# A hybrid S5 / Conformer layer on one core: every other gate weight tile moved into an 8 KB buffer and prepared a tile ahead, and the rest of the adaLN modulation computed as rows

## Chip, core and metric

The kernel is written in Bass/Tile and runs on one core of one Trainium2 chip. The metric is the device time of one execution in microseconds. The engines are called PE (TensorE, matrix products), DVE (VectorE), ACT (ScalarE), POOL (GpSimd) and SP (SyncE, which here only issues DMAs; ACT issues the stores).

## What is computed

One layer of a network on 2048 tokens of 1024 channels, with a context prefix of 256 tokens, all in float32. Cut to what matters for the change:

```python
mod = silu(c) @ ada_w + ada_b                 # 6 parts of 1024: sh1 sc1 g1 sh2 sc2 g2
nl  = modulate(rmsnorm(x, norm1_g), sh1, sc1)
zl  = nl @ w_in          # 512 S5 input | 1024 conv GLU input | 2048 branch gate logits
ys  = s5_mixer(zl[:, :512], ...)              # bidirectional state-space scan, 32 groups
ya  = s5_glu_out(ys, w_glu, w_a)
yb  = conformer_branch(zl[:, 512:1536], ...)  # a*sigmoid(b), conv of width 31, LayerNorm, silu, @ w_b
x   = x + g1 * (sigmoid(ga) * ya + sigmoid(gb) * yb) @ w_out
nl2 = modulate(rmsnorm(x, norm2_g), sh2, sc2)
out = rmsnorm(x + g2 * conv_ffn(nl2, w_up, dw, w_down), final_g)
```

## The kernel before

A float32 product is made of three PE products of rounded halves: `split` (L446 to L453) rounds an operand to a high half (a cast on ACT, L449) and takes the rest as a low half (a subtraction on DVE, L453), and `mm3` (L459 to L464) multiplies high by high (L462), high by low (L463) and low by high (L464). A tile of 128 output channels by 512 tokens takes 8 slices of the contraction, so 24 matmuls of 512 columns; a tile of 128 channels over all 2048 tokens is four such blocks.

The program runs in stages: the first modulation parts and the S5 input (0 to about 345 us), then the conv GLU tiles and the gates with the S5 scans and the convolution behind them (to about 850 us), the two branch outputs and the merge (phase 3a, 850 to 1150 us), the output projection, and the FFN (1330 us to the end).

**Gates and GLU tiles (L826 to L872).** `v_pair(ct)` computes one channel tile of the conv GLU: four blocks whose sigmoid goes into a tile `av` (L840, ACT), then four blocks that are multiplied into it (L847, DVE), and a store of `av` to DRAM on ACT's queue (L849). `gate(m)` computes one channel tile of gate logits, takes its sigmoid and stores it. The order is v_pair(0), gates 0 to 2, v_pair(1), gates 3 to 5, v_pair(2), gates 6 and 7, v_pair(3), gates 8 to 13; gates 14 and 15 come last with a pool of their own (`ring2`).

**Weights.** `wtile` (L498 to L510) loads two pieces of 256 KB into `w_raw` (three buffers, on SP, L496), and splits each into a `w_ch` of the pool `ring`, which has three slots. A weight tile takes two of the three, so of the next tile one half can be prepared, and the other waits until PE has read the first half of the present one for the last time.

**The S5 in the background (L337 to L412).** After each block of 24 matmuls a `background` call lets the S5 generator take three steps and the convolution 0.75 of one. For each of 32 groups SP loads a record `grp` of three parts (L348, L349, L350); two matmuls read it (L385), POOL and DVE rotate and scan (L394 to L397, L408, L410), POOL rotates back (L361 to L364), and three kinds of matmul read out (L368 to L370). The convolution reads `av` back from DRAM (`caw`, L784, on SP) with its weights `ctw` (L781).

**Buffers.** Tiles of 8 KB per partition share one tag, `z8`, with eight buffers. During the gates four hold a normalised input block; the other four serve `av` and `grp`. A tile takes the buffer that came free longest ago, in program order, and the loads of SP stand in one queue, so a load that waits for its buffer holds up all that stand behind it.

**Rest of the modulation (L890 to L937).** The last four parts are done in phase 3a: `ada_rest` loads `ada_w` in slabs (L924) and accumulates them on DVE (L928); `collect` (L901 to L917) sums over the 128 partitions with PE. Parts 0 and 3 (the two gates g1, g2) come as a row: one matmul with a vector of ones over 512 columns (L907), the bias loaded as a row (L908), an addition (L909) and a store to the DRAM row `d_row` (L910). Parts 1 and 2 (shift and scale of the second modulation) come as columns: four matmuls of one column each (L913) and one addition (L917).

The lines which the diff touches, and the gate loop that calls them:

Of the kernel before, what the change touches and what calls it, by code (L numbers as in the profile page):

```python
# [9 lines left out]
F32 = mybir.dt.float32  # L10
F32R = mybir.dt.float32r
I32 = mybir.dt.int32
AF = mybir.ActivationFunctionType
OP = mybir.AluOpType
# [3 lines left out]
D = 1024  # L18
SEQ = 2048
# [411 lines left out]
class Net:  # L431
# [91 lines left out]
    def run(self):  # L523
        nc, tc = self.nc, self.tc
        with ExitStack() as ctx:
            self.cp = cp = ctx.enter_context(tc.tile_pool(name="const", bufs=1))
            dp = ctx.enter_context(tc.tile_pool(name="scratch", bufs=1, space=DRAM))
            dt_ = lambda nm, sh: dp.tile(sh, F32, name=nm)
            self.scr = {
                "rec": dt_("d_rec", [G, 128, 512 + 2 * NX]), "kd": dt_("d_kd", [G, H, 2 * T - 1, H]),  # L530
                "u": dt_("d_u", [G, H, T, NX]), "y": dt_("d_y", [G, H, T, NCL]),
                "sg": dt_("d_sg", [2, 8, 128, SEQ]), "cv": dt_("d_cv", [4, 128, CS, CX]),
                "av": [dt_(f"d_av{i}", [128, CS, CX]) for i in range(4)],
                "mg": [dt_(f"d_mg{b}", [8, 128, 512]) for b in range(4)], "h": dt_("d_h", [16, 128, D]),
                "hid": dt_("d_hid", [22, 128, SEQ]), "row": dt_("d_row", [2, D]),
                "m8": cp.tile([128, G], F32, name="m8"),
            }
            cp.tile([128, 8], F32, name="align")
            self.big = ctx.enter_context(tc.tile_pool(name="big", bufs=1))
            self.phase1()  # L540
            self.phase3b_4()
            self.phase5()
# [54 lines left out]
    def phase1(self):  # L597
        nc, tc, ins, scr, v, a = self.nc, self.tc, self.ins, self.scr, self.v, self.a
        w_in = ins["w_in"]
        with ExitStack() as ctx:  # L600
            psum = ctx.enter_context(tc.tile_pool(name="ps1", bufs=4, space=PSUM))
            up = ExitStack()
            ring = up.enter_context(self.pool("ringu", 8))
# [148 lines left out]
            ring = ringx.enter_context(self.pool("ring", 3))  # L752
# [3 lines left out]
            stage = []  # L756
# [52 lines left out]
            def background(nconv=None, ns5=None):  # L809
                if nconv is None:  # L810
                    nconv = 0.75
                if ns5 is None:
                    ns5 = 3.0
                pace[0] += nconv
                while pace[0] >= 1.0:
                    pace[0] -= 1.0
                    while fill:
                        try:
                            next(fill[0])
                            break  # L820
                        except StopIteration:
                            fill.pop(0)
                pace[1] += ns5
                while pace[1] >= 1.0:
                    pace[1] -= 1.0
                    next(s5, None)  # L826
# [3 lines left out]
            def v_pair(ct):  # L830
# [18 lines left out]
                self.store(scr["av"][ct], av)  # L849
                fill.append(conv_rows(ct))  # L850

            def gate(m, order=(0, 1, 2, 3), w=None):
                w = w or self.wtile(ring, w_in, 1536 + 128 * m)
                for b in order:
                    ps = psum.tile([128, 512], F32, name="ps", tag="mm")
                    self.gemm(ps, w, x_of(b))
                    sg = evp.tile([128, 512], F32, name="sgg", tag="ev")
                    with self.urgent():
                        a.activation(sg, ps, AF.Sigmoid)
                    self.store(scr["sg"][m // 8][m % 8][:, 512 * b:512 * b + 512], sg)  # L860
                    background()

            m = 0
            for ct in range(4):
                v_pair(ct)
                for _ in range((3, 3, 2, 0)[ct]):
                    gate(m)
                    m += 1
            while m < 14:
                gate(m)  # L870
                m += 1
# [21 lines left out]
    def ada_rest(self, psum, fp):  # L893

        v, cp, pe = self.v, self.cp, self.pe
        self.A2 = cp.tile([128, 8], F32, name="A2")
        self.S2 = cp.tile([128, 8], F32, name="S2")
        ar = Arena([self.z8("ada", [128, 2048])])
        accs, slabs = [ar(128, 512) for _ in range(2)], [ar(128, 512) for _ in range(2)]

        def collect(j, acc):  # L901
            c0 = 2048 + 512 * j
            part, hf = j // 2, j % 2
            ps = psum.tile([128, 512], F32, name="ps", tag="mm")
            if part in (0, 3):
                row = fp.tile([1, 512], F32, name="adrow")
                pe.matmul(ps[0:1, :], self.ones[:, 0:1], acc, start=True, stop=True)  # L907
                self.dma(row, self.ins["ada_b"][None, c0:c0 + 512])  # L908
                v.tensor_tensor(row, row, ps[0:1, :], op=OP.add)  # L909
                self.dma(self.scr["row"][part // 3:part // 3 + 1, 512 * hf:512 * hf + 512], row)  # L910
            else:
                for i in range(4):
                    pe.matmul(ps[:, i:i + 1], acc[:, 128 * i:128 * i + 128], self.ones[:, 0:1],  # L913
                              start=True, stop=True)
                dst = self.S2 if part == 1 else self.A2
                i0 = c0 // 128
                v.tensor_tensor(dst[:, 4 * hf:4 * hf + 4], ps[:, :4], self.col["ab"][:, i0:i0 + 4], op=OP.add)  # L917

        for j in range(8):
            c0 = 2048 + 512 * j  # L920
            acc = accs[j % 2]
            for k in range(8):
                sl = slabs[k % 2]
                self.dma(sl, self.ins["ada_w"][128 * k:128 * k + 128, c0:c0 + 512])  # L924
                if k == 0:
                    v.tensor_scalar(acc, sl, self.sc[:, 0, 0:1], None, op0=OP.mult)
                else:
                    v.scalar_tensor_tensor(acc, sl, self.sc[:, k, 0:1], acc, op0=OP.mult, op1=OP.add)  # L928
                if k % 2:
                    yield  # L930
                if k == 5 and j:
                    collect(j - 1, accs[(j - 1) % 2])
        yield
        yield
        collect(7, accs[1])
        v.scalar_tensor_tensor(self.A2, self.A2, 1.0, self.col["n2"], op0=OP.add, op1=OP.mult)
        yield  # L937
# [329 lines left out]
    def phase5(self):  # L1267
        nc, tc, ins, scr, v, a = self.nc, self.tc, self.ins, self.scr, self.v, self.a
        RES = 18
        with ExitStack() as ctx:  # L1270
# [5 lines left out]
            g2 = op_.tile([128, D], F32, name="g2row", bufs=1)  # L1276
# [39 lines left out]
            def down(t0, nt, nlast):  # L1316

                n = 128 * nt
                acc = [[psum.tile([128, 512], F32, name="ps", tag="mm") for _ in range(2)] for _ in range(nt)]

                pair = []

                def operand(k):
                    hr = hp.tile([128, n], F32, name="hr", bufs=2)
                    self.dma(hr, scr["hid"][k][:, 128 * t0:128 * t0 + n])
                    if not pair:
                        t = hp.tile([128, 2, 512], F32R, name="hhl")
                        pair.extend(t[:, :, o:o + n] for o in range(0, 512, n))
                    ht = pair.pop(0)
                    self.split(ht[:, 0], ht[:, 1], hr)  # L1330
                    return ht, wk(k)

                def step(x, j, hf, i):
                    (ht, w), js = x, slice(128 * j, 128 * j + 128)
                    self.mm3(acc[j][hf], (ht[:, 0, js], ht[:, 1, js]), w[hf], i == 0, i == 21)

                for i, k in enumerate(ORDER[:22 - nlast]):
                    x = operand(k)
                    for j in range(nt):
                        for hf in range(2):  # L1340
                            step(x, j, hf, i)
                if t0 == 0:
                    self.dma(fg, ins["final_g"][None, :].to_broadcast([128, D]))
                    self.dma(g2, scr["row"][1:2, :].to_broadcast([128, D]))
                xs = [operand(k) for k in ORDER[22 - nlast:]]
                for j in range(nt):
                    for hf in range(2):
                        for i, x in enumerate(xs):
                            step(x, j, hf, 22 - nlast + i)
                    residual(t0 + j, acc[j])  # L1350

            for t0, nt, nlast in ((0, 4, 2), (4, 4, 2), (8, 4, 2), (12, 2, 2), (14, 2, 6)):
                down(t0, nt, nlast)
# [58 lines left out]
```

## Time and profile before

| | |
|---|---|
| three runs, median (lowest to highest) | 2812.69 us (2808.87 to 2816.03) |
| the profiled execution's own time | 2806.18 us |
| its span | 2804.4 us |
| mean granted PE clock | 0.984 of full speed |
| PE busy | 2711.9 us, 97% of the span, 12044 matmuls |
| DVE busy | 1508.0 us, 54% |
| ACT busy | 822.7 us, 29% |
| POOL busy | 459.3 us, 16% (nearly all of it before 850 us) |
| chain that ended last | PE 75%, DVE 9%, DMA 6%, POOL 5% |

PE is busy for 97% of the span, and of the rest only a part lies in the two stages that the change touches. The rows below therefore look at single waits of PE in the stretch of the gates, and at the queues on which those waits hang. In a timeline row the first number is the start and the second the duration in microseconds; a bracket at the end gives the idle time of the engine before the row and what ended it. A matmul row lasts longer than the distance to the next start, since matmuls overlap.

### The profile page before, as it was taken

To read this page: it belongs to the slowest core of one execution; us is meant where nothing else is said; L and a number is where in the kernel's file an instruction comes from. 1 tells how busy PE (TensorE), PEld (TensorE's weight loads), DVE (VectorE), ACT (ScalarE), POOL (GpSimd) and SP (SyncE) were. 2 spreads that over 40 slices of the span, in tenths; PEclk is the share of its full clock that TensorE was granted. 3 is DMA by queue.
4 is the path that set the end of the run, shared out by engine and by line. 5 is a ranking of instruction groups with operands and counts; after the bars stand their busy time and mean duration, and the time that the engine had idled before them with its cause. 6 is when DMAs were issued, how large, how long until landed. Compare 5 with 4: busy or idle time off the path is not lost.

```text
span 2804.4 us, 32119 instructions
## 1 busy us (share of the span) xinstructions
PE 2711.9 (97%) x12044; PEld 2203.2 (79%) x12044; DVE 1508.0 (54%) x2312; ACT 822.7 (29%) x1446; POOL 459.3 (16%) x504
## 2 busy tenths in 40 slices
PE   7998999999999999999999999999999989999998
PEld 3786878788887777788888888888888878787887
DVE  5867643433316788566855646556465462414154
ACT  2555412121235443243421222212222132212122
POOL 2256477667600000000000000000000000000000
PEclk8999999999999999999999999999999999999999
DMA  8645745354436576533111111111111153323143
GB/s 315 195 142 165 205 138 153 126 177 147 145 102 202 173 206 200 187 131 113 64 46 57 42 49 49 49 53 46 45 57 42 53 179 107 113 71 135 53 143 98
DMA packets 327308, 334.73 MB, mean 119 GB/s; under 512 B 95336, under 2 KB 240360, under 8 KB 324464
## 3 DMA queue, kind: packets, MB, share of 16 engines
q1 hardware_dynamic: 245680, 235.13, 27.2%
q10 hardware_dynamic: 81472, 97.54, 10.0%
q8 instruction: 95, 1.56, 0.2%
q14 instruction: 61, 0.50, 0.1%
HBM read 230.38 MB, written 102.21 MB: 119 GB/s over the span
## 4 chain that ended last, share of the span: by engine, by line
PE 75%; DVE 9%; DMA 6%; POOL 5%; issue 2%; ACT 2%; SPq 0%; ACTq 0%; POOLq 0%; DVEq 0%
PE ps L464 23%; PE ps L462 23%; PE ps L463 23%; DMA sgab<-d_sg 2%; PE ps L795 1%; DVE Hs L408 1%; PE ps L577 1%; PE ps L385 1%; POOL t L395 1%; DVE Hs L410 1%; DMA slab<-in_ada_w_dram 1%; DMA ada<-in_ada_w_dram 1%; POOL t L394 1%; POOL t L361 1%; PE ps L1112 0%
## 5 line engine op out<-in xcount | busy, mean ns | idle before, releaser
L1242 DVE SCALAR_TENSOR_TENSOR acc<-pad,fw,acc 128x1024 f32<-128x1024 f32 x352 | 450.4, 1282 | 238.9 <-ACT acc L1238 229.5
L477 POOL TENSOR_TENSOR rs_y<-rs_v,mhalf 128x1 f32<-128x1 f32 (+1 forms) x41 | 27.4, 668 | 2048.8 <-DVE rs_v L476 2048.8
L462 PE MATMUL ps<-wd,hhl 128*128 128x512 f32 x704 | 275.6, 393 | 13.5 <-ACT hhl L449 7.3
L463 PE MATMUL ps<-wd,hhl 128*128 128x512 f32 x704 | 275.7, 392 | 0.0
L464 PE MATMUL ps<-wd,hhl 128*128 128x512 f32 x704 | 275.3, 392 | 0.1
L408 DVE TENSOR_TENSOR_SCAN Hs<-m,S 64x287 f32<-64x287 f32 x64 | 68.8, 1075 | 240.5 <-POOL S L396 240.1
L453 DVE TENSOR_TENSOR hhl<-hr,hhl 128x512 fp32r<-128x512 f32 (+1 forms) x110 | 63.0, 582 | 244.4 <-ACT hhl L449 244.1
L453 DVE TENSOR_TENSOR w_ch<-w_raw,w_ch 128x512 fp32r<-128x512 f32 x134 | 106.4, 801 | 137.9 <-ACT w_ch L449 137.5
L462 PEld LDWEIGHTS ps<-wd,hhl 128*128 128x128 f32 x704 | 133.2, 189 | 43.3 <-ACT hhl L449 7.9
L449 ACT CAST w_ch<-w_raw 128x512 fp32r<-128x512 f32 x142 | 87.6, 621 | 267.2 <-PE ps L464 167.1
L463 PEld LDWEIGHTS ps<-wd,hhl 128*128 128x128 f32 x704 | 133.2, 189 | 28.6 <-DVE wd L453 1.0
L464 PEld LDWEIGHTS ps<-wd,hhl 128*128 128x128 f32 x704 | 133.1, 189 | 28.5 <-DVE hhl L453 0.8
L449 ACT CAST hhl<-hr 128x512 fp32r<-128x512 f32 (+1 forms) x110 | 57.2, 534 | 264.5 <-PE ps L464 231.3
L463 PE MATMUL ps<-nm2l,w_ch 128*128 128x512 f32 x344 | 133.8, 389 | 0.0
L464 PE MATMUL ps<-nm2h,w_ch 128*128 128x512 f32 x344 | 133.8, 389 | 0.0
L462 PE MATMUL ps<-nm0h,w_ch 128*128 128x512 f32 x344 | 133.8, 389 | 0.0
L463 PE MATMUL ps<-nm0l,w_ch 128*128 128x512 f32 x344 | 133.8, 389 | 0.0
L463 PE MATMUL ps<-nm1l,w_ch 128*128 128x512 f32 x344 | 133.8, 389 | 0.0
L463 PE MATMUL ps<-nm3l,w_ch 128*128 128x512 f32 x344 | 133.8, 389 | 0.0
L464 PE MATMUL ps<-nm0h,w_ch 128*128 128x512 f32 x344 | 133.8, 389 | 0.0
L462 PE MATMUL ps<-nm1h,w_ch 128*128 128x512 f32 x344 | 133.8, 389 | 0.0
L464 PE MATMUL ps<-nm1h,w_ch 128*128 128x512 f32 x344 | 133.8, 389 | 0.0
(370 smaller groups left out, 6354.5 us busy)
## 6 DMA issues: line engine op xcount, KB each, us to landing
w_raw<-in_ffn_w_up_dram SPq DMA_DIRECT2D x88, 256.0 KB
d_hid<-acc ACTq DMA_DIRECT2D x88, 256.0 KB
w_raw<-in_ffn_w_down_dram SPq DMA_DIRECT2D x76, 256.0 KB
grp<-d_rec SPq DMA_DIRECT2D x32, 576.0 KB
hr<-d_hid SPq DMA_DIRECT2D x66, 256.0 KB
d_sg<-sgg ACTq DMA_DIRECT2D x64, 256.0 KB
ada<-in_ada_w_dram SPq DMA_DIRECT2D x64, 256.0 KB
sgab<-d_sg SPq DMA_DIRECT2D x32, 512.0 KB
```

The costliest lines, as they stand in the source:

```text
L361: g_.tensor_tensor(r1, Hl, tb[:, 0:1, LAT].to_broadcast([128, 2, NCL]), op=OP.mult)
L385: nc.tensor.matmul(ps[:, :NX], sm[:, i, :], ug, start=True, stop=True)
L394: g_.tensor_tensor(t1, S, tb[:, 0:1, :].to_broadcast([128, 2, NX]), op=OP.mult)
L395: g_.tensor_tensor(t2, S[:, ::-1, :], tb[:, 1:2, :].to_broadcast([128, 2, NX]), op=OP.mult)
L408: v.tensor_tensor_scan(Hs[0:64, i, 1:1 + nsc], mb[0:64], S[0:64, i, 0:nsc], 0.0, op0=OP.mult, op1=OP.add)
L410: v.tensor_tensor_scan(Hs[64:128, i, NX - 1 - nsc:NX - 1][:, ::-1], mb[64:128], S[64:128, i, NX - nsc:NX][:, ::-1], 0.0, op0=OP.mult, op1= ...
L449: self.a.copy(hi, src)
L453: e.tensor_tensor(lo, src, hi.bitcast(F32), op=OP.subtract)
L462: mm(ps, wh, xh, start=first, stop=False)
L463: mm(ps, wh, xl, start=False, stop=False)
L464: mm(ps, wl, xh, start=False, stop=last)
L1242: v.scalar_tensor_tensor(acc[:, h], win(h, t // 3, t % 3), fw[:, i, t:t + 1], acc[:, h], op0=OP.mult, op1=OP.add)
```

## The change

Two parts. First, from the moment that the S5 main generator starts (`stage` set, during v_pair(1)), the weight tiles of odd gates no longer go into `ring` but into one `z8` tile, split with the same priority as before; and the tile of an odd gate is requested before the matmuls of the even gate ahead of it. Gate 3 is the first odd gate after that moment and is requested at its own start; 5, 7, 9, 11 and 13 a gate ahead. Second, `collect` computes parts 1 and 2 as rows too, stores them in `d_row` (now four rows), and SP reads each half back as four columns of `S2` or `A2`.

```diff
-                "hid": dt_("d_hid", [22, 128, SEQ]), "row": dt_("d_row", [2, D]),
+                "hid": dt_("d_hid", [22, 128, SEQ]), "row": dt_("d_row", [4, D]),
...
+            gw = {}
+
+            def gate_weights(m):
+
+                c0 = 1536 + 128 * m
+                if m % 2 == 0 or not stage:
+                    gw[m] = self.wtile(ring, w_in, c0)
+                    return
+                t = self.z8("w_ch", [128, 2, 8, 128], F32R)
+                f = "p k c -> p (k c)"
+                for q in range(2):
+                    raw = self.raw_tile(w_in[512 * q:512 * q + 512, c0:c0 + 128].rearrange("(k p) c -> p k c", p=128))
+                    with self.urgent():
+                        self.split(t[:, 0, 4 * q:4 * q + 4].rearrange(f), t[:, 1, 4 * q:4 * q + 4].rearrange(f), raw)
+                gw[m] = [(t[:, 0, k], t[:, 1, k]) for k in range(8)]
+
             def gate(m, order=(0, 1, 2, 3), w=None):
-                w = w or self.wtile(ring, w_in, 1536 + 128 * m)
+                if w is None:
+                    if m not in gw:
+                        gate_weights(m)
+                    w = gw.pop(m)
+                    if m + 1 < 14 and (m + 1) % 2 and stage:
+                        gate_weights(m + 1)
...
-            if part in (0, 3):
-                row = fp.tile([1, 512], F32, name="adrow")
-                pe.matmul(ps[0:1, :], self.ones[:, 0:1], acc, start=True, stop=True)
-                self.dma(row, self.ins["ada_b"][None, c0:c0 + 512])
-                v.tensor_tensor(row, row, ps[0:1, :], op=OP.add)
-                self.dma(self.scr["row"][part // 3:part // 3 + 1, 512 * hf:512 * hf + 512], row)
-            else:
-                for i in range(4):
-                    pe.matmul(ps[:, i:i + 1], acc[:, 128 * i:128 * i + 128], self.ones[:, 0:1],
-                              start=True, stop=True)
-                dst = self.S2 if part == 1 else self.A2
-                i0 = c0 // 128
-                v.tensor_tensor(dst[:, 4 * hf:4 * hf + 4], ps[:, :4], self.col["ab"][:, i0:i0 + 4], op=OP.add)
+            row = fp.tile([1, 512], F32, name="adrow")
+            pe.matmul(ps[0:1, :], self.ones[:, 0:1], acc, start=True, stop=True)
+            self.dma(row, self.ins["ada_b"][None, c0:c0 + 512])
+            v.tensor_tensor(row, row, ps[0:1, :], op=OP.add)
+            dst = self.scr["row"][part:part + 1, 512 * hf:512 * hf + 512]
+            self.dma(dst, row)
+            if part in (1, 2):
+                col = self.S2 if part == 1 else self.A2
+                self.dma(col[:, 4 * hf:4 * hf + 4], dst.rearrange("o (a p) -> p (o a)", p=128))
...
-                    self.dma(g2, scr["row"][1:2, :].to_broadcast([128, D]))
+                    self.dma(g2, scr["row"][3:4, :].to_broadcast([128, D]))
```

A scheduler places the instructions on the engines' queues, so the change also moves some that it does not name. Three places follow.

**SP, at the load of S5 group 5, during the last block of v_pair(1).** `grp_3510` before and `grp_3509` after are the record of group 5; `w_raw` are weight pieces of w_in, `caw` the convolution's reads of the stored `av` of v_pair(1). Before:

```order
L348 DMA grp_3510<-d_u_62 128x1x320
L349 DMA grp_3510<-d_rec_60 128x1152
L350 DMA grp_3510<-d_kd_61 128x1x128
L496 DMA w_raw_3981<-in_w_in_dram 128x4x128
L496 DMA w_raw_3986<-in_w_in_dram 128x4x128
L784 DMA caw_3554<-d_av1_67 128x1x128 x2
L784 DMA caw_3618<-d_av1_67 128x1x128 x2
```

With the change:

```order
L496 DMA w_raw_3729<-in_w_in_dram 128x4x128
L496 DMA w_raw_3733<-in_w_in_dram 128x4x128
L496 DMA w_raw_4234<-in_w_in_dram 128x4x128
L496 DMA w_raw_4239<-in_w_in_dram 128x4x128
L348 DMA grp_3509<-d_u_62 128x1x320
L349 DMA grp_3509<-d_rec_60 128x1152
L350 DMA grp_3509<-d_kd_61 128x1x128
L784 DMA caw_3553<-d_av1_67 128x1x128 x2
L784 DMA caw_3617<-d_av1_67 128x1x128 x2
```

The group's load moved behind four weight loads; the buffer that it had is taken by gate 3's weights, and it now gets the buffer of `av` of v_pair(1). Group 17, after v_pair(2), moves in the same way onto the buffer of that `av`; group 27, after v_pair(3), onto the third `av`'s buffer and behind two `caw` loads. On PE the two matmuls of L385 for group 5 stand 13 matmuls later than before and those of group 17 ten later; otherwise PE's order before 850 us is the same but for one statistics matmul of phase 3a's first block near its end.

**DVE, around the last multiplication into `av` of v_pair(1).** `av_3037` is that tile, the `w_ch` rows are the low halves of weight tiles, `Hs` an S5 scan. Before:

```order
L847 TENSOR_TENSOR av_3037<-ps_3371,av_3037 128x16x32
L453 TENSOR_TENSOR w_ch_3472<-w_raw_3470,w_ch_3472 128x512
L847 TENSOR_TENSOR av_3037<-ps_3419,av_3037 128x16x32
L453 TENSOR_TENSOR w_ch_3721<-w_raw_3719,w_ch_3721 128x512
L408 SCALAR_TENSOR_TENSOR Hs_3514<-m8_77,S_3445 64x287
```

With the change:

```order
L847 TENSOR_TENSOR av_3037<-ps_3371,av_3037 128x16x32
L453 TENSOR_TENSOR w_ch_3465<-w_raw_3466,w_ch_3465 128x512
L453 TENSOR_TENSOR w_ch_3465<-w_raw_3470,w_ch_3465 128x512
L453 TENSOR_TENSOR w_ch_3725<-w_raw_3723,w_ch_3725 128x512
L847 TENSOR_TENSOR av_3037<-ps_3419,av_3037 128x16x32
L453 TENSOR_TENSOR w_ch_4236<-w_raw_4234,w_ch_4236 128x512
```

Three subtractions instead of one stand between the last two multiplications; the same holds for the `av` of v_pair(2), and not for that of v_pair(3).

**SP in phase 3a, at the first half of part 1.** `ada` are slabs of ada_w, `sgab` the stored gates of a merge tile. Before:

```order
L1051 DMA sgab_7907<-d_sg_64 128x2x512
L951 DMA yr_8154<-d_y_63 128x8x64 x2
L924 DMA ada_7205<-in_ada_w_dram 128x512 x2
L1051 DMA sgab_7944<-d_sg_64 128x2x512
L924 DMA ada_7205<-in_ada_w_dram 128x512 x2
```

With the change (the lines of the later code are 17 higher):

```order
L1068 DMA sgab_7902<-d_sg_64 128x2x512
L968 DMA yr_8150<-d_y_63 128x8x64 x2
L931 DMA d_row_76<-adrow_7879 1x512
L941 DMA ada_7199<-in_ada_w_dram 128x512 x2
L934 DMA S2_7198<-d_row_76 128x4x1
L928 DMA adrow_8031<-in_ada_b_dram 1x512
L1068 DMA sgab_7939<-d_sg_64 128x2x512
```

Four times in phase 3a the store of a row, the read-back of four columns and the load of the next bias row now stand in SP's queue, the read-back two slab loads behind the store that it reads.

## Rows read from the trace of the kernel before

**Rows 1.** PE's waits by releaser, 350 to 850 us: total, times, longest.

```profile
PE ps L464 <- DVE w_ch L453: 8.2, 4, 3.5
PE ps L369 <- POOL S L363: 3.9, 3, 2.0
PE ps L462 <- ACT w_ch L449: 1.2, 1, 1.2
PE ps L385 <- DMA grp<-d_rec: 1.0, 1, 1.0
```

**Rows 2.** PE's timeline, the wait in v_pair(1)'s second tile.

```profile
369.93 0.50 PE L464 MATMUL ps<-nl0h,w_ch 128*128 128x512 f32 x1 [3.50 <-DVE w_ch L453]
```

**Rows 3.** PE's timeline, v_pair(2)'s first tile and S5 group 12.

```profile
494.32 0.39 PE L462 MATMUL ps<-nl0h,w_ch 128*128 128x512 f32 x1
494.54 0.39 PE L463 MATMUL ps<-nl0l,w_ch 128*128 128x512 f32 x1
497.03 0.50 PE L464 MATMUL ps<-nl0h,w_ch 128*128 128x512 f32 x1 [2.10 <-DVE w_ch L453]
...
506.52 1.34 PE L385 MATMUL ps<-grp 128*128 128x320 f32 x4 [1.02 <-DMA grp<-d_rec]
```

**Rows 4.** Windows of 20 us: busy by engine, granted clock, DMA share, GB/s.

```profile
370.00:390.00 20.00, 20.00 (x81) 16.29 (x82) 6.52 (x7) 1.60 (x4) 16.48 (x15) 0.91 0.36 115
490.00:510.00 20.00, 16.88 (x69) 13.16 (x68) 6.06 (x8) 3.02 (x7) 9.65 (x10) 0.91 0.50 155
550.00:570.00 20.00, 17.95 (x78) 14.32 (x77) 10.73 (x12) 4.38 (x9) 13.31 (x13) 1.00 0.66 217
```

**Rows 5.** PE's timeline, the S5 group matmuls: groups 4 (readout), 5, 17 and 27.

```profile
401.93 0.97 PE L385 MATMUL ps<-grp 128*128 128x320 f32 x3
...
410.38 0.70 PE L369 MATMUL ps<-S,grp 128*128 128x256 f32 x2 [1.29 <-POOL S L363]
...
560.83 0.97 PE L385 MATMUL ps<-grp 128*128 128x320 f32 x3
...
692.84 1.24 PE L385 MATMUL ps<-grp 128*128 128x320 f32 x4
```

**Rows 6.** SP's timeline: group 5's load, and the first `caw` after each `av`.

```profile
389.39 0.45 SPq L349 DMA_DIRECT2D grp<-d_rec  x1
...
401.69 2.53 SPq L784 DMA_DIRECT2D caw<-d_av  x4
...
561.16 2.51 SPq L784 DMA_DIRECT2D caw<-d_av  x4
...
688.54 2.47 SPq L784 DMA_DIRECT2D caw<-d_av  x4
```

**Rows 7.** The critical chain, 480 to 570 us: start, length, what.

```profile
500.41 6.06 DMA grp<-d_rec
```

**Rows 8.** DMA throughput, 389 to 397 us, in slices of 0.2 us.

```profile
GB/s 0 0 0 0 0 64 19 13 38 128 174 252 406 279 343 234 387 451 364 305 230 312 207 210 166 146 67 36 3 0 0 41 0 0 0 0 0 0 0 0
```

**Rows 9.** DVE's timeline, one weight subtraction at the end of v_pair(1).

```profile
394.71 1.34 DVE L453 TENSOR_TENSOR w_ch<-w_raw,w_ch 128x512 fp32r<-128x512 f32 x1
```

**Rows 10.** PE's timeline in phase 3a: a row group and a column group.

```profile
946.27 1.02 PE L907 MATMUL ps<-ada,ones 128*1 128x512 f32 x2
947.22 0.50 PE L462 MATMUL ps<-tgl,wa 128*128 128x512 f32 x1
...
998.47 0.95 PE L913 MATMUL ps<-ones,ada 128*128 128x1 f32 x8
999.28 0.48 PE L462 MATMUL ps<-sln,wb 128*128 128x512 f32 x1
```

**Rows 11.** SP's waits by releaser, 850 to 1150 us: total, times, longest.

```profile
SPq L924 <- DVE ada L928: 60.7, 45, 5.1
...
SPq L910 <- DVE adrow L909: 5.4, 4, 3.2
```

**Rows 12.** DVE's addition to a row in phase 3a: min/median/max ns.

```profile
L909 DVE TENSOR_TENSOR adrow<-adrow,ps x4: 665/669/676, 950.7 to 1125.9; 1x512 f32<-1x512 f32 x4
```

## Prediction

> **What bounds the kernel now.** Read PE's waits first [rows 1], then where they stand, then the queue that ends each. PE works nearly all the time; between 350 and 850 us, the stretch of the first part of the change, it idles only 14.3 us in all: 8.2 for weight tiles that DVE has not finished, 3.9 for POOL's rotation before an S5 readout, 1.2 for a weight cast, 1.0 for an S5 record. That, and what the clock loses behind the waits, is all that this part can win. The longest weight wait is 3.50 us at 369.93, in v_pair(1)'s second tile [rows 2]; the next is 2.10 us at 497.03, in the first tile of v_pair(2) [rows 3]. The other two, 2.6 us together, stand in the second tiles of v_pair(2) and v_pair(3). None stands in a gate from 3 to 13, so the tiles that the change prepares ahead are not the ones that are late.
>
> Two of these waits cost more than their length. In each of the windows 370 to 390 and 490 to 510 us the granted clock is 0.91, where the window 550 to 570 us, which holds the POOL wait of 2.0 us, has 1.00 [rows 1, 4]. [...] The trace thus shows the loss behind waits of 2.10 and 3.50 us and not behind one of 2.0.
>
> **Part one, what it removes.** With gate 5 out of the ring, v_pair(2)'s first tile finds free slots earlier, its subtractions come before the scans that hold them up now, and SP does not stand at their loads when group 12's record is due. That takes away 2.10 us, the 1.8 us of clock behind it, and the wait of 1.02 us for the record at 506.52 [rows 3]: −4.9 us. Group 12's load is then held only by convolution weights, and lands before PE asks. The cast wait of 1.2 us [rows 1] is at the last gates, whose tiles are cast earlier now: −1.2. The waits in the second tiles of v_pair(1), (2) and (3) stay: the scans stand ahead of their subtractions on DVE as before, and gate 3's own tile is ready by its start.
>
> **What it adds.** Of the four buffers that `av` and the S5 records share, `w_ch` takes one. Three records lose their place and wait for the `av` store to land, with PE in order behind them:
>
> Group 5. Its record was requested at 389.39 [rows 6] and used at 401.93 [rows 5]. Now it needs the buffer of v_pair(1)'s `av`. That store has landed at 401.69, when the `caw` load that reads it goes out [rows 6]. Three subtractions in place of one now stand ahead of the last multiplication into `av`; one takes up to 1.34 us there [rows 9], so the store is 0 to 2.7 us later. I take 2.5, since DVE is the engine that finishes that tile. A group's first part takes about 0.6 us to issue. The record itself took 6.06 us in one place [rows 7] and, in a quiet one, from its issue at 389.39 to the end of the transfers in slice 28, at 394.6, so 5.2 us [rows 6, 8]. I take 5.2, the shorter. So it lands at 401.7 + 2.5 + 0.6 + 5.2 = 410.0. PE reaches the matmuls 13 places later than before; matmuls start 0.22 us apart [rows 3], so at 401.93 + 2.9 = 404.8. The wait is 5.2 us; it absorbs the wait of 1.29 us for POOL that follows at 410.38 [rows 5], as POOL runs on meanwhile: **+3.9** (with 0 and 2.7 for the subtractions and 5.2 and 6.06 for the record: 1.4 to 5.0).
>
> Group 17. The same after v_pair(2): store landed at 561.16 [rows 6], record there at 561.2 + 2.5 + 0.6 + 5.2 = 569.5, PE at 560.83 [rows 5] plus ten matmuls, 563.0. Of 6.5 us, the POOL wait of 2.0 [rows 1] is absorbed: **+4.5** (2.0 to 5.6).
>
> Group 27. Its load follows two `caw` loads, half of the 2.47 us from 688.54 [rows 6]: 688.5 + 1.2 + 0.6 + 5.2 = 695.5, against 692.84 [rows 5]: **+2.7** (2.7 to 3.6).
>
> All three waits are longer than 2.10, so each gets the loss of clock, 3 × 1.8 = **+5.4** (0 to 5.4). [...]
>
> The other records come closer to their use too, but keep 37 matmuls or more in the order, some 8 us: nothing.
>
> **Part two.** On PE four groups of eight short column matmuls (998.47 to 999.28, 0.81 us) become four of two row passes (946.27 to 947.22, 0.95 us) [rows 10]: 4 × 0.14 = **+0.6**. DVE's addition takes 0.67 us [rows 12] instead of one over four columns, at most +2.7 on an engine that is not the bound: nothing. SP gets four bias loads, four stores and four read-backs more. The store waits for DVE's addition, 5.4 us over four times now [rows 11], and behind it stand gate loads of the merge and slabs. But SP waits 60.7 us for slab buffers in this stretch [rows 11], time in which an earlier issue would have gained nothing, so I take 0; below 0 nothing excludes −1 from the reshuffled matmuls, and if every new row held SP for the longest of those waits, 3.2 us, and half came through, it is 6.
>
> **Sum.** 3.9 + 4.5 + 2.7 + 5.4 + 0.6 − 4.9 − 1.2 = +11.0 us. Against the profiled execution of 2806.2 us, which lies 6.5 below the median of the runs, that is 2817.2; against the median of 2812.7 it is **2823.7 us**. The bounds give −0.5 to +20: 2812 to 2833. A measurement of this kernel can tell about 0.3%, 8.4 us, from no change.
>
> **Rivals.**
> *The records come in time (0.17).* If SP issues them sooner, because the store lands sooner or the load takes half as long, as two of the three would have to, only −4.9 − 1.2 + 0.6 = −5.5 is left: 2807 us, no change to measure. Against: 9 matmuls between request and use, 2 us, was all that the new order leaves groups 5 and 17, and no record in [rows 7, 8] took under 5.
>
> *All weight waits go (0.12), faster.* The ring is free every second tile, so both halves of every v_pair tile could be split before PE comes. What decides is whether their subtractions pass the S5 scans in DVE's queue. Were that so and the records in time, 8.2 + 1.2 + 1.0 and two losses of clock, 3.6, less 0.6, would go: −13.4, 2799 us. For it speaks 497.03, where this happens; against it that PE's wait of 3.50 is on a tile split before the change begins, and that the DVE order keeps the scans first at the other two.
>
> *The read-back holds SP (0.08), slower still.* The read-back must wait until its store has landed, and two slab loads are all the cover. If the gate loads behind it are late, +6 on top: 2830 us. Against: SP's idle time above. [...]
>
> *The change does nothing that counts (0.05).* The waits that it adds fall into POOL's and DVE's waits, which move along: 2813 us.
>
> **Chances.** The forecast's own case has 0.58; of it 0.42 over 8.4 us and 0.16 below, where the stores are no later and some of the clock holds. Slower 0.42 + 0.08 = 0.50; within 0.3% 0.16 + 0.17 + 0.05 = 0.38; faster 0.12. The range from 2806 to 2832 takes in all but the faster rival and the upper ends.
>
> **What would show it.** In the profile after: PE waits at L385 for `grp<-d_rec` rise from 1.0 to some 14 us, in three pieces near 405, 565 and 693; behind each the clock is granted at half for some us; the POOL waits near 410 and 569 are gone; the weight wait at 497 and the record's wait behind it are gone, those at 370, 529 and 656 stay. Phase 3a shows the four new rows and no new wait of PE over 1 us. Wrong it would be if the three records stand on time, or if SP's queue in phase 3a shows PE waiting for `sgab` or slabs.

## The result

The changed kernel takes 2830.2 us (median of 6 runs, 2826.17 to 2835.08), before 2815.84 us (median of 6, the three of the table above among them, 2808.87 to 2818.39). The ratio is 1.0056, 95% interval 1.0045 to 1.0068: slower by 14 us between the medians, by some 16 by the ratio. The profiled execution of the change took 2835.08 us, the highest of its six, with a span of 2833.3 us; that of before, 2806.18 us, lies under all six of its runs. So the two profiles are further apart (28.9 us) than the two kernels.

PE does nearly the same work and is a smaller share of a longer span:

```profile
PE 2719.8 (96%) x12020; PEld 2202.9 (78%) x12020; DVE 1511.1 (53%) x2312; ACT 819.1 (29%) x1444; POOL 460.1 (16%) x504
```

PE's waits by releaser between 350 and 860 us (total, times, longest) answer to [rows 1]:

```profile
PE ps L385 <- DMA caw<-d_av: 9.1, 1, 9.1
PE ps L464 <- DVE w_ch L453: 8.9, 5, 3.5
PE ps L385 <- DMA grp<-d_rec: 6.8, 2, 5.0
PE ps L369 <- POOL S L363: 1.3, 2, 0.7
```

L385 is the first product on an S5 record. Its wait was 1.0 us and is now 9.1 + 6.8 = 15.9. (The first is put down to a `caw` load, since the profile names the transfer that ended last by its records; L385 reads no `caw`.) The weight waits have not shrunk. The cast wait of 1.2 us is gone.

PE's timeline shows the places; the lines behind the first of the three show the slower clock:

```profile
399.68 0.50 PE L464 MATMUL ps<-nl0h,w_ch 128*128 128x512 f32 x1 [1.68 <-DVE w_ch L453]
...
418.34 2.47 PE L385 MATMUL ps<-grp 128*128 128x320 f32 x4 [9.09 <-DMA caw<-d_av]
...
421.47 0.63 PE L462 MATMUL ps<-nl1h,w_ch 128*128 128x512 f32 x1
421.89 0.63 PE L463 MATMUL ps<-nl1l,w_ch 128*128 128x512 f32 x1
...
423.60 0.46 PE L464 MATMUL ps<-nl1h,w_ch 128*128 128x512 f32 x1
...
578.42 2.47 PE L385 MATMUL ps<-grp 128*128 128x320 f32 x4 [5.01 <-DMA grp<-d_rec]
...
584.10 0.43 PE L462 MATMUL ps<-nl1h,w_ch 128*128 128x512 f32 x1
...
710.50 1.31 PE L385 MATMUL ps<-grp 128*128 128x320 f32 x4 [1.75 <-DMA grp<-d_rec]
```

The waits at L385 are those of groups 5, 17 and 27; the first line is gate 3's tile. Until 423.6 matmuls start 0.42 us apart instead of 0.22 [rows 3]: from the end of the wait at 418.34 that is 5.3 us at the lower level (granted clock 0.50 from 418.4 to 423.6), about 2.6 us lost. Behind the second wait it is 5.7 us, until 584.10 (0.50 from 578.4 to 584). The windows of 20 us (columns as in [rows 4]: PE first, clock third from the end):

```profile
410.00:430.00 20.00, 11.66 (x39) 9.17 (x40) 6.30 (x8) 2.17 (x5) 9.36 (x9) 0.74 0.58 168
490.00:510.00 20.00, 20.00 (x101) 16.91 (x101) 7.38 (x11) 3.44 (x9) 13.54 (x12) 1.00 0.46 131
570.00:590.00 20.00, 14.99 (x54) 11.58 (x53) 7.30 (x8) 2.63 (x6) 12.81 (x13) 0.83 0.61 205
700.00:720.00 20.00, 18.25 (x86) 14.99 (x85) 7.71 (x8) 4.87 (x11) 16.20 (x15) 1.00 0.72 242
```

The clock falls around groups 5 and 17 (0.74, 0.83) and not at group 27, whose wait is 1.75 us (1.00). In 490 to 510 us, where before idled and lost clock, PE is now busy throughout. The same matmuls stand some 12 us later in this profile, and it does neither there: PE's list of waits from 420 to 535 us is empty, and the window 510 to 530 us has 20.00 and 1.00. The gain of the change is there.

The chain of waits between 396 and 420 us (start, length, what) tells why group 5 is 9 us late:

```profile
397.70 0.69 DVE av L847
398.39 4.08 DVE w_ch L453 x3
...
402.49 5.89 DMA w_raw<-in_w_in_dram
...
408.40 0.63 ACT w_ch L449
...
409.05 0.70 DVE w_ch L453
...
409.77 0.37 SPq L496
...
410.23 5.69 DMA grp<-d_u
```

Three subtractions give back a raw weight buffer at 402.5; the load that takes it is cast and subtracted at 409.05; only then has SP a buffer for the fourth weight load of its queue (the fourth L496 of the first list "With the change"), at 409.77, and the record behind it goes out at 410.2. The `av` store whose buffer the record takes was issued at 403.09:

```profile
403.09 0.34 ACTq L849 DMA_DIRECT2D d_av<-av  x1
...
410.88 0.44 SPq L349 DMA_DIRECT2D grp<-d_rec  x1
```

In before, the load behind such a store went out 5.0, 5.1 and 5.9 us after the store's issue, so this one had landed by about 409 (an estimate) and was not the last to be waited for. It was not far from it: the record went out 1 to 2 us after that. At group 17 it is the store: issued at 567.81 on ACT's queue, and SP free to load 5.57 us later:

```profile
567.81 0.33 ACTq L849 DMA_DIRECT2D d_av<-av  x1
...
573.38 0.60 SPq L348 DMA_DIRECT2D grp<-d_u  x1
```

The read-back of part two does not hold SP's queue: the first of the four goes out right behind the two slab loads that cover its store, and the longest gap ahead of one of the others is 0.8 us.

```profile
1028.96 0.26 SPq L931 DMA_DIRECT2D d_row<-adrow  x1
1029.62 1.60 SPq L941 DMA_DIRECT2D ada<-in_ada_w_dram  x2
1031.27 0.43 SPq L934 DMA_DIRECT2D S<-d_row  x1
```

### The profile page after: what moved, and what is told of

Read it like the earlier page. It is cut to its first block, busy times and chain, and to the rows that moved or that the text cites. A ratio compares the mean times of both kernels' runs of the same rounds, so it can differ in the third digit from the quotient of the medians.

```text
span 2833.3 us, 32109 instructions
## 1 busy us (share of the span) xinstructions
PE 2719.8 (96%) x12020; PEld 2202.9 (78%) x12020; DVE 1511.1 (53%) x2312; ACT 819.1 (29%) x1444; POOL 460.1 (16%) x504
## 3 DMA queue, kind: packets, MB, share of 16 engines
q8 instruction: 94, 1.54, 0.2%
## 4 chain that ended last, share of the span: by engine, by line
PE 71%; DMA 9%; DVE 9%; POOL 4%; issue 3%; ACT 2%; SPq 1%; ACTq 0%; POOLq 0%; DVEq 0%
PE ps L464 23%; PE ps L462 23%; PE ps L463 22%; DMA sgab<-d_sg 2%; DMA w_raw<-in_w_in_dram 1%; PE ps L795 1%; DMA ada<-in_ada_w_dram 1%; DVE Hs L408 1%; POOL t L395 1%; PE ps L385 1%; DVE Hs L410 1%; DVE w_ch L453 1%; PE ps L1129 0%; DVE ada L945 0%; POOL t L394 0%
## 5 line engine op out<-in xcount | busy, mean ns | idle before, releaser
L462 PE MATMUL ps<-wd,hhl 128*128 128x512 f32 x704 | 275.6, 393 | 14.4 <-ACT hhl L449 9.6
L462 PE MATMUL ps<-nm3h,w_ch 128*128 128x512 f32 x344 | 133.8, 389 | 0.0
```

The lines of the kernel that those rows point to most:

```text
L462: mm(ps, wh, xh, start=first, stop=False)
```

## The experiments

A number used below: the S5 stretch, from PE's first L385 to its last L370, lasts 417.0 us before (347.5 to 764.6) and 433.7 us with the change (349.8 to 783.5). All of the first part's gains and losses but the last gates lie in it.

| kernel | time against before, 95% | S5 stretch, us | PE's waits there for records, weights, POOL, us |
|---|---|---|---|
| before | 1 | 417.0 | 1.0, 8.2, 3.9 |
| the change | 1.0056 (1.0045 to 1.0068) | 433.7 | 15.9, 8.9, 1.3 |
| e1: gates alone | 1.0055 (1.0041 to 1.0070) | 432.2 | 15.5, 9.4, 1.3 |
| e2: rows alone | 1.0006 (0.9998 to 1.0015) | 417.0 | 0.9, 8.2, 4.0 |
| e3: gate 3 in the ring | 1.0014 (1.0003 to 1.0025) | 421.7 | 6.9, 7.9, 2.6 |
| e4: nothing ahead | 1.0032 (1.0020 to 1.0044) | 427.3 | 8.5, 7.6, 5.2 |
| e5: gate 5 alone | 0.9985 (0.9975 to 0.9994) | 413.2 | 0, 6.1, 4.0 |
| e7: e5, low halves on POOL | 0.9986 (0.9978 to 0.9995) | 412.2 | 0, 1.5, 6.4 |
| e8: gates 5 and 13 | 0.9981 (0.9971 to 0.9990) | 413.3 | 0, 6.1, 5.1 |

**e1, the gates alone.** The diff above without its parts on `d_row`, `collect` and `g2`.

> The first part alone: odd gates' weight tiles in an 8 KB buffer and requested a gate ahead; the modulation as before. Theory (late S5 records carry the whole loss): the three waits of PE for records, 9.1, 5.0 and 1.8 us with the change, stand here unchanged, and the time is that of the change within 3 us, so some 12 to 16 us over before. Rival (the read-back of columns holds up SP's queue in phase 3a): the time is under 9 us over before and the rest belongs to the second part.

The time is that of the change. PE's waits in e1, 345 to 860 us:

```profile
PE ps L385 <- DMA grp<-d_rec: 15.5, 3, 8.3
PE ps L464 <- DVE w_ch L453: 9.4, 5, 3.5
PE ps L369 <- POOL S L363: 1.3, 3, 0.6
```

The three waits are 8.3, 5.1 and 2.1 us. The loss belongs to the first part, and in it to the S5 stretch (+15.2 us of a measured 1.0055, 15.5 us).

**e2, the rows alone.** Only the parts on `d_row`, `collect` and `g2`.

> The second part alone: shift and scale of the second modulation as rows, read back as columns; the gates as before. Theory: within 3 us of before, PE's waits between 850 and 1160 us within 3 us of the 17 us of before. Rival (the read-back holds SP's queue): 5 us or more over before, and PE waits there for the merge or for a tile whose load stands behind the read-back.

Between 0.6 us under and 4.2 us over before: nothing that the measurement can tell. But PE's waits from 850 to 1160 us are 23.0 us, where before has 17.1, further off than the 3 us expected, and phase 3a looked longer than that of before: from PE's first product on a gelu block to the first of the output projection, in e2

```profile
884.59 0.39 PE L462 MATMUL ps<-gh,wglu 128*128 128x512 f32 x1
...
1154.32 0.76 PE L462 MATMUL ps<-wo,mhl 128*128 128x512 f32 x1 [4.54 <-DVE mg L1056]
```

it is 269.7 us, where the first profile of before has 263.1, from 884.67 to 1147.72. So before was profiled again (e6).

**e6, before once more.** No edit.

> The kernel before, unchanged, for a second profile of it. Theory (the 5 to 6 us that phase 3a is longer in the profile of the second part alone are scatter from run to run): phase 3a, from the first matmul on a gelu block to the first of the output projection, lasts 266 us or more where the first profile had 263. Rival (they are the read-back): it lasts 262 to 264 us again.

```profile
884.12 0.39 PE L462 MATMUL ps<-gh,wglu 128*128 128x512 f32 x1
...
1151.68 0.57 PE L462 MATMUL ps<-wo,mhl 128*128 128x512 f32 x1 [2.94 <-DVE mg L1060]
```

Here it is 267.6 us, at a time of 2813.13 us, near the median, and PE's waits are 21.6 us. The stage scatters by some 4 us from execution to execution, and the first profile of before had a short one. But scatter is not all. In the eight profiles without the rows (before twice, e1, e3, e4, e5, e7, e8) the stage lasts 263.1 to 267.6 us, 266.0 on average; in the two with them it lasts 269.7 (e2) and 271.1 us (the change), the longest of the ten. By these profiles the rows make the stage some 4 us longer, about the most that the timed runs leave room for. The wait for the merge that ends it is 4.5 and 3.9 us with the rows and 2.5 to 3.3 without, and DVE is busy for 208.4 us in the stage where the others have 205.3 to 206.3, about the +2.7 that the prediction gave the additions. Which of these lengthens the stage is not shown.

**e3, gate 3 in the ring.**

```diff
-                if m % 2 == 0 or not stage:
+                if m % 2 == 0 or m < 5 or not stage:
```

> The first part without gate 3: gates 5, 7, 9, 11 and 13 as in the change, gate 3 in the ring. Theory (gate 3's tile takes the buffer that group 5's record had): the wait of 9.1 us at group 5 goes, the records of groups 17 and 27 still come late by about 5 and 2 us, the wait at v_pair(2)'s first tile stays away; together 0 to 5 us over before. Rival (the weight pieces of gate 5, requested ahead, hold SP's queue whoever has the buffer): a wait of 4 us or more for group 5's record stays.

```profile
PE ps L464 <- DVE w_ch L453: 7.9, 5, 3.5
PE ps L385 <- DMA grp<-d_rec: 6.9, 2, 5.1
PE ps L369 <- POOL S L363: 2.6, 3, 1.3
```

Group 5's wait is gone, and so is the weight wait at gate 3's start; the other two records wait 5.1 and 1.85 us, in e1 5.1 and 2.05. The S5 stretch falls by 10.5 us against e1 and the time to 1.0014. Of the steps of the change that were taken out singly, gate 3's tile in the shared buffers was the dearest.

**e4, nothing ahead.** Each odd gate's tile is requested at its own start.

```diff
                     w = gw.pop(m)
-                    if m + 1 < 14 and (m + 1) % 2 and stage:
-                        gate_weights(m + 1)
```

> The first part with each odd gate's tile requested at its own start and not a gate ahead. Theory (two causes at group 5: the buffer, and gate 5's pieces which hold two of three raw buffers and with them SP): group 5's wait shrinks from 9.1 to some 5 us, what the landing of the av store alone costs, the waits at groups 17 and 27 go, as the request no longer comes before their loads; 0 to 5 us over before. Rival (the buffer alone): group 5's wait stays near 9 us and the time is 5 to 10 us over before.

```profile
PE ps L385 <- DMA grp<-d_rec: 8.5, 1, 8.5
PE ps L464 <- DVE w_ch L453: 7.6, 4, 3.5
PE ps L369 <- POOL S L363: 5.2, 4, 2.2
```

Half right. Groups 17 and 27 are on time: there, asking a gate ahead took the buffer. Group 5 still waits 8.5 us, so the theory that gate 5's early request was what held SP's queue falls. The rival named the size but not the whole reason: SP's queue of e4 has four weight loads ahead of group 5 as well (397.84 to 408.44). By the program's order they are two of gate 5 and two of v_pair(2), for with an odd gate out of the ring the ring is free early; the trace does not say whose pieces they are. Four pieces for three raw buffers hold SP whoever asked first. The queue is the smaller part of the wait, though: the record's first part goes out 7.2 us after the `av` store (401.29 to 408.53), where loads behind a store alone went 5.0 to 5.9 us after it, so the queue has 1.3 to 2.2 of the 8.5 us (an estimate), and the store alone would leave more than the theory's 5.

**e5, gate 5 alone.** The change's gain is in the tile ahead of v_pair(2). Gate 5 alone frees the ring there; its request at its own start leaves the buffers of groups 5, 17 and 27 as they were.

```diff
-                if m % 2 == 0 or not stage:
+                if m != 5:
...
                     w = gw.pop(m)
-                    if m + 1 < 14 and (m + 1) % 2 and stage:
-                        gate_weights(m + 1)
```

> Of the change only this: gate 5's tile in an 8 KB buffer, requested at its own start; every other gate in the ring, the modulation as before. Theory (the gain comes from the ring being free ahead of v_pair(2), the loss from records that lose their buffer): no record comes late, PE's waits of 2.1 us at v_pair(2)'s first tile and of 1.0 us for group 12's record go, the stretch of the S5 lasts 412 us where before has 417; 3 to 7 us under before. Rival (whatever takes one of the four shared buffers makes some record late): a wait of 2 us or more for a record appears and the time is not below before.

```profile
PE ps L464 <- DVE w_ch L453: 6.1, 3, 3.5
PE ps L369 <- POOL S L363: 4.0, 3, 2.0
PE ps L462 <- ACT w_ch L449: 1.2, 1, 1.2
```

No record is late, the two waits near 500 us are gone, the stretch is 3.8 us shorter and the time 0.15% (0.06 to 0.25) lower, 4.2 us. That is the prize of the change without its price. The clock is no part of the gain in this profile: from 450 to 580 us it is 0.99 in both. The loss near 500 us is gone (485 to 505 us: 0.91 in before; in e5 the block matmuls from 492.56 to 502.12 start 0.22 to 0.24 us apart), but one has come behind a POOL wait that before has with full clock and in the same length (565 to 585 us: 1.00 in before; in e5 matmuls start 0.42 to 0.43 us apart from 567.29 to 569.42).

```profile
565.24 0.70 PE L369 MATMUL ps<-S,grp 128*128 128x256 f32 x2 [2.05 <-POOL S L363]
...
567.29 0.63 PE L463 MATMUL ps<-nl2l,w_ch 128*128 128x512 f32 x1
```

**e7, the low halves of the v_pair tiles on POOL.** The remaining weight waits are in tiles whose first half ACT had cast 8 to 10 us before DVE came to its subtraction, behind four scans (in before the casts start at 358.16, 519.68 and 645.78, the subtractions at 369.19, 528.27 and 655.14). With e5's edit:

```diff
+                self.low = "g"
                 w = self.wtile(ring, w_in, 512 + 128 * ct)
+                self.low = "v"
```

> As the run with gate 5 alone, and the low halves of the second weight tile of each v_pair are subtracted on POOL instead of DVE. Theory (PE's waits in those tiles are the order of DVE's queue, four scans ahead of a subtraction whose cast was done long before): PE's waits for weight tiles fall from some 6 us to under 2, and the clock loss behind the 3.5 us goes too; 10 to 15 us under before. Rival (POOL is what bounds the S5 there and has no room): its waits before readouts grow by as much, and the time is that of the run with gate 5 alone or above.

```profile
PE ps L369 <- POOL S L363: 6.4, 5, 3.0
PE ps L464 <- POOL w_ch L453: 1.5, 1, 1.5
PE ps L462 <- ACT w_ch L449: 1.2, 1, 1.2
```

The weight waits do fall, from 6.1 to 1.5 us, so DVE's order was their cause. But POOL pays: its timeline has the subtraction at 1.71 us, followed by the S5's rotations,

```profile
366.85 1.71 POOL L453 TENSOR_TENSOR w_ch<-w_raw,w_ch 128x512 fp32r<-128x512 f32 x1
370.84 1.70 POOL L361 TENSOR_TENSOR t<-Hs,grp 128x512 f32<-128x512 f32 x1 [2.28 <-DVE Hs L410]
```

and PE waits 2.4 us more before readouts, up to 3.0 at one. The stretch is 1.0 us shorter and the time equals e5's. Nor does the clock come back: from 350 to 450 us it is 0.98 in before, in e5 and here. Behind the weight wait, now 1.54 us at 368.61, matmuls start 0.22 to 0.24 us apart, but behind the POOL wait of 2.99 us at 374.61 they start 0.42 to 0.43 us apart from 376.63 to 378.77, and so they do from 530.93 to 532.21. The theory's 10 to 15 us are not there; the rival, that the S5 behind the gates takes back what PE saves, is the nearer one.

**e8, gates 5 and 13.** As e5 with `m not in (5, 13)`.

> As the run with gate 5 alone, and gate 13's tile too in an 8 KB buffer, requested at its own start, when the S5 has ended and no record can be late. Theory (the cast wait at the last gates comes from gate 13 in the ring): the wait of 1.2 us of PE for a weight cast goes, all else as with gate 5 alone, so 4 to 7 us under before. Rival (the last gates' casts are late for another reason): the wait of 1.2 us stays, and the time is that of gate 5 alone.

```profile
PE ps L464 <- DVE w_ch L453: 6.1, 3, 3.5
PE ps L369 <- POOL S L363: 5.1, 4, 2.0
```

The cast wait at the last gates is gone from the list, as with the change: it came from gate 13 in the ring. The time is 0.19% (0.10 to 0.29) under before, 5.3 us: the fastest version of this study, faster than both kernels, though not separable from e5.

## Why the prediction was right, and where it was off

The forecast was 11 us slower with range 2806 to 2832 us; measured are 2830.2 us, 14 us slower by the medians and some 16 by the ratio, and the mechanism is the one that it named: late records. In the S5 stretch its terms were 5 us too low together, and two of its sums fit in part by chance.

**The gain near 500 us: right.** −4.9 was forecast. From 425 to 535 us PE has no wait and the clock is at 1.00; e5, which keeps this gain and nothing that makes a record late, is 4.2 us faster. The cast wait, −1.2, goes too, and e8 shows that gate 13 is its cause.

**The three late records: right in place, and in sum partly by chance.** Forecast 5.2, 6.5 and 2.7 us, together 14.4; measured 9.1, 5.0 and 1.8, together 15.9. The step that failed is "lands at 401.7 + 2.5 + 0.6 + 5.2": it took the landing of the `av` store for what holds group 5's record, and 5.2 us for the record itself. In the chain the fourth weight load ahead of the record in SP's queue comes last, which went out 7.3 us after the load before it (402.49 to 409.77), when a raw buffer came free. The order list ahead of the prediction showed those four loads; the prediction counted the group's buffer and not theirs. How the 3.9 us between 5.2 and 9.1 divide can be counted from the last multiplication but one into `av`, at 397.70 with the change and at 394.10 before:

```profile
394.10 0.69 DVE L847 TENSOR_TENSOR av<-ps,av 128x512 f32<-128x512 f32 x1
...
396.68 0.34 ACTq L849 DMA_DIRECT2D d_av<-av  x1
```

The store goes out 5.4 us behind it instead of 2.6, so 2.8 us later, where 2.5 was forecast. The record's first part goes out 7.1 us after the store (403.09 to 410.23), where `caw` went 5.0 after it in before: about 2.1 us for the queue, 1.2 with the longest of before's stores. From there to PE's start at 418.34 it is 8.1 us, where 0.6 + 5.2 was forecast: 2.3 us. PE comes 0.8 us later than forecast, which shortens the wait. So with a clear queue group 5 would still have waited some 7 to 8 us (an estimate; no run has it). Why the record took longer is not shown: from the issue of its second part to PE's start it is 7.5 us here, 6.5 and 6.8 in e1 and e4, and 4.4 at group 17. The waits of groups 17 and 27 were 1.5 and 0.9 us shorter than forecast, which hides part of this in the sum; group 17 was held by the store's landing alone.

**The absorbed POOL waits: right.** 3.3 us were to be absorbed, 2.6 were (3.9 to 1.3).

**Gate 3's own tile: wrong.** "Ready by its start" was the text; in fact PE waits 1.68 us at 399.68 and, after v_pair(2), 1.16 at 567.24, since the three subtractions that delay the store also delay each other behind the scans. Forecast for the stretch's weight waits was −2.1, measured +0.7.

**The clock: right in sum, by chance.** Forecast 3 × 1.8 = 5.4 us. The 1.8 us are 0.09 of a window of 20 us behind each of two waits in before [rows 4]; in the first of these the granted clock is 0.56, 0.50, 0.50 and 0.73 in the four microseconds from 371, which is 1.7 us. That a wait longer than 2.10 us always brings this loss was the author's estimate, and no run shows the 1.8 behind a late record. Measured: the waits of 9.1 and 5.0 us cost 2.6 and 2.8 (half of 5.3 and 5.7 us at a granted clock of 0.50; the windows of groups 5 and 17 have 0.74 and 0.83), that of 1.75 nothing (700 to 720 us: 1.00), where the forecast had a wait of 2.7 and a loss. The forecast read full clock behind the POOL wait of 2.0 us from the window 550 to 570 us, which ends where the wait does; the window behind it, 570 to 590 us, has 1.00 as well.

Together: 15.9 − 1.0 for records, +0.7 for weights, −2.6 for POOL, and 5.4 − 1.8 for the clock make +16.6 for the stretch, and the profiles give 433.7 − 417.0 = 16.7. The forecast's terms for it made +11.6. Of the 5.0 between them weights have 2.8 (gate 3's tile and the wait after v_pair(2)), records 1.5 (group 5's 3.9 less what groups 17 and 27 fell short) and POOL 0.7.

**Part two: right within what the timed runs can tell.** +0.6 forecast, 1.7 measured (−0.6 to 4.2). Phase 3a itself is some 4 us longer in both profiles with the rows (see e6), more than the +0.6, and the cause stays open. The rival of a held SP queue does not show: no read-back has a gap of more than 0.8 us ahead of it, and PE waits 0.5 us for `sgab` in e2 and 0.6 in e6.

**The rivals.** That the records come in time is refuted by every profile with gate 3 out of the ring. That all weight waits go is refuted by the change's own 8.9 us; e7 adds that removing most of them by moving the work to POOL does not make the time lower than e5's. That the change does nothing that counts is refuted by the interval of 1.0045 to 1.0068.

## What to carry to other kernels

A buffer taken from a shared pool was paid here by the load that used to get it, group 5's record, whose wait of 9.1 us is gone in e3: follow the order in which the tiles are given out and look at every load that now waits for another release, and at every load ahead of it in its queue. Count the raw buffers of the loads that move forward too, because with gate tiles out of the ring four weight loads stood ahead of that record, where before had none. Where the gain is one wait, free the resource at that place alone: here one of six tiles brought all of the gain near 500 us; gate 3's tile and the requests a gate ahead brought the loss.

## What was not expected of the hardware

Behind PE's waits of about 2 us the clock went either way: the window behind 2.10 us in before has a clock of 0.91 [rows 3, 4], and those of e1 behind 2.08 us (390 to 405) and 2.05 us (700 to 720) have 1.00. Even the same wait does both: behind the POOL wait of 2.05 us the clock stays at 1.00 in before (565 to 585 us), and in e5 matmuls behind it start 0.42 to 0.43 us apart; the wait of 3.50 us in v_pair(1) has 0.91 in before and 1.00 in e1 (360 to 380 us). So the length of a wait does not settle it in these profiles. A forecast that gives each such wait the full loss, as this one did for group 27, is too high by a part that these runs do not settle. The same subtraction of a weight half on DVE took 0.69 us at 409.05 and 1.3 to 1.4 each at 398.39 (4.08 for three); POOL's rotations and sums ran beside the three (397.81 to 403.06) and none beside the one at 409.05; that they are the cause is not shown.
